# Mixture of softmaxes on one core: which output groups wait behind the last load, and where they wait

## The chip, the core and the metric

The kernel runs on one core of a Trainium2 chip. The metric is device time in microseconds (us) of one execution. Engines are PE (matmul; PEld is its weight load), DVE (vector), ACT (scalar), POOL (GpSimd) and SP (sync). Transfers between HBM (the chip's main memory) and SBUF (on-chip memory of 128 partitions) are issued by SP and ACT in this kernel. Each of the two has its own queue, and both queues are served by the same 16 transfer engines.

## The reference, cut to what matters

```
prior_probs = softmax(prior, axis=-1)              # [32, 128, 4]
softmax     = softmax(logits, axis=-1)             # [32, 128, 4, 4096]
mixture     = sum over 4 heads of prior_probs[..., None] * softmax
```

The logits are 268 MB of float32, the output is 67 MB. For each of 4096 rows there are four heads of 4096 logits each. The result is one row of 4096 numbers: the four softmaxes, weighted by the softmax of four prior numbers.

## The kernel before, in words

**Tiling.** The 4096 rows are cut into G = 32 groups of 128 rows, and each group into J = 2 units of M = 64 rows, so there are N = 64 units. Unit n is half j = n % 2 of group n // 2. The four heads of a unit's 64 rows lie on 128 partitions: partition 2m + q holds heads 2q and 2q + 1 of row m, as two stretches of 4096 (Q = 2, index i). A unit is 4 MB, 32 KB on each partition.

**Loads.** `load(n)` (L66 to L72) is issued by SP, as one transfer of 4 MB; unit 63 alone is loaded as two of 2 MB. `slot(n)` (L63, L64) says in which of five slot tiles a unit lies: slot n % 5, except for the last six units, which go to slots 4, 0, 1, 2, 4, 0. Slot 3 is thus last read by unit 53. A slot can be loaded again when the matmuls of its earlier unit are done.

**Arithmetic of a unit.** `top(n, i)` (L74 to L81) takes the maximum of a stretch on DVE (L76) and then the exponential with its sum on ACT (L79), in place. `weigh(n, i)` (L83 to L98) takes the reciprocal of the sum on DVE (L84), builds on POOL (L86) a 128 x 64 matrix which adds the two partitions of a row, weighted by prior and reciprocal, and runs 16 matmuls (L93). They add both stretches of the unit into one PSUM tile of 128 x 2048: partitions 0 to 63 hold output columns 0 to 2047, partitions 64 to 127 columns 2048 to 4095. `evict(n)` (L112, L113) copies that on ACT to the home of the group, once its matmuls are done.

**Homes and stores.** `home(g)` (L108 to L110) is where the sums of group g wait: half g % 2 of the output tile `obuf`, or of slot 3 for the two held groups, 28 and 29 (`HOLD` = 28, L106). `part` (L100 to L104) stores one half c of the partitions of a group, which is one half of its columns: 1 MB in pieces of 8 KB. Up to group 27, `store(g)` issues both halves on ACT as soon as the group's second unit has been copied (L174, L175).

**Order of the work.** The order is written out by hand; every engine takes its instructions in the order in which the loop names them. Step n of the loop (L155 to L179) does: the maximum and exponential of unit n's first stretch; the second `weigh` of unit n - 1; the load into the slot that unit n - 1 frees; maximum and exponential of the second stretch of unit n, and its first `weigh`; the copy of unit n - 1; and the stores that follow from it.

**The end.** At step 62 the held groups are stored: their upper halves (c = 1) by ACT, after the first exponential of unit 62 (L158 to L160), their lower halves (c = 0) by SP, behind the two halves of load 63 in SP's queue (L166 to L168). Groups 30 and 31 go the same two ways: group 30 after the copy of unit 61, the first half of group 31 after that of unit 62 (L176 to L179), and the last unit in two pieces of 1024 columns, each copied and stored on both queues (L183 to L186).

**Semaphores.** Completions of transfers are counted on eight semaphores in turn, shared by both queues. So an engine that issues a transfer may first have to wait for an earlier transfer that used the same semaphore; the list of built instructions shows where it does.

Of the kernel before, what the change touches and what calls it, by code (L numbers as in the profile page):

```python
# [17 lines left out]
SLOTS = 5  # L18


@with_exitstack
def kernel(
    ctx: ExitStack,
    tc: tile.TileContext,
    logits: bass.AP,
    prior: bass.AP,
    out: bass.AP,
):
    nc = tc.nc
    B, S, H, V = logits.shape  # L30
    R = M * J
    G = B * S // R
    N = G * J
    W = V // 2
    assert G * R == B * S and G == 32 and H == 2 * Q and V == 8 * BANK


    lg = logits.rearrange("b s h v -> (b s) h v").rearrange(
        "(g m j) (q i) v -> g j m q (i v)", m=M, j=J, i=Q
    )  # L40
    ov = out.rearrange("b s v -> (b s) v").rearrange("(g m j) v -> g m j v", m=M, j=J)
    pv = prior.rearrange("b s h -> (b s) h").rearrange("(g r) h -> g r h", r=R)

    cpool = ctx.enter_context(tc.tile_pool(name="cpool", bufs=1))
    psum = ctx.enter_context(tc.tile_pool(name="psum", bufs=1, space=bass.MemoryType.PSUM))

    slots = [cpool.tile([P, Q, V], FP32, name=f"slot{i}") for i in range(SLOTS)]

    obuf = cpool.tile([P, J, V], FP32, name="obuf")
    accs = [psum.tile([P, W], FP32, name=f"acc{i}") for i in range(2)]  # L50

    sel = cpool.tile([P, M], FP32, name="sel")
    wts = [[cpool.tile([P, M], FP32, name=f"wt{k}{i}") for i in range(Q)] for k in range(2)]
    pr = cpool.tile([G, R, H], FP32, name="pr")
    pn = cpool.tile([G, J, Q, M, Q], FP32, name="pn")
    pmax = cpool.tile([G, R], FP32, name="pmax")
    pp = cpool.tile([P, J, Q, G], FP32, name="pp")
    nmax = [cpool.tile([P, N], FP32, name=f"nmax{i}") for i in range(Q)]
    dsum = [cpool.tile([P, N], FP32, name=f"dsum{i}") for i in range(Q)]
    rden = [cpool.tile([P, N], FP32, name=f"rden{i}") for i in range(Q)]  # L60


    def slot(n):  # L63
        return slots[n % SLOTS if n < N - 6 else (4, 0, 1, 2)[(n - N + 6) % 4]]  # L64

    def load(n):  # L66
        src = lg[n // J, n % J]
        for i in range(0, Q, Q if n < N - 1 else 1):
            k = Q if n < N - 1 else 1
            nc.sync.dma_start(  # L70
                out=slot(n)[:, i : i + k], in_=src[:, :, i * V : (i + k) * V]
            )  # L72

    def top(n, i):  # L74
        x = slot(n)[:, i]
        nc.vector.tensor_reduce(  # L76
            out=nmax[i][:, n : n + 1], in_=x, axis=AX.X, op=ALU.max, negate=True
        )
        nc.scalar.activation(  # L79
            x, x, AF.Exp, bias=nmax[i][:, n : n + 1], accum_out=dsum[i][:, n : n + 1]  # L80
        )  # L81

    def weigh(n, i):  # L83
        nc.vector.reciprocal(rden[i][:, n : n + 1], dsum[i][:, n : n + 1])  # L84
        wt = wts[n % 2][i]
        nc.gpsimd.tensor_scalar(  # L86
            out=wt, in0=sel, scalar1=rden[i][:, n : n + 1],
            scalar2=pp[:, n % J, i, n // J : n // J + 1], op0=ALU.mult, op1=ALU.mult,
        )

        for b in range(W // BANK):
            for c in range(2):
                nc.tensor.matmul(  # L93
                    accs[n % 2][c * M : (c + 1) * M, b * BANK : (b + 1) * BANK],
                    lhsT=wt,
                    rhs=slot(n)[:, i, c * W + b * BANK : c * W + (b + 1) * BANK],
                    start=i == 0, stop=i == Q - 1,
                )  # L98

    def part(eng, g, c, js=slice(0, J), lo=0, hi=W):  # L100
        eng.dma_start(  # L101
            out=ov[g, :, js, c * W + lo : c * W + hi],
            in_=home(g)[c * M : (c + 1) * M, js, lo:hi],
        )  # L104

    HOLD = G - 4  # L106

    def home(g):  # L108
        x = slots[3] if HOLD <= g < G - 2 else obuf
        return x[:, g % 2].rearrange("p (j w) -> p j w", j=J)  # L110

    def evict(n, lo=0, hi=W):  # L112
        nc.scalar.copy(home(n // J)[:, n % J, lo:hi], accs[n % 2][:, lo:hi])  # L113

    def store(g):
        for c in range(2):
            part(nc.scalar, g, c)

    def prior_user(n):
        return max(k for k in range(n) if slot(k) is slot(n))  # L120

    with tc.manual_schedule():
        for n in range(SLOTS):
            load(n)
        nc.scalar.dma_start(out=pr, in_=pv)

        nc.gpsimd.memset(sel, 1.0)  # L127
        nc.gpsimd.affine_select(  # L128
            out=sel, in_=sel, compare_op=ALU.is_ge, fill=0.0, base=0,
            pattern=[[-Q, M]], channel_multiplier=1,  # L130
        )
        nc.gpsimd.affine_select(  # L132
            out=sel, in_=sel, compare_op=ALU.is_ge, fill=0.0, base=Q - 1,
            pattern=[[Q, M]], channel_multiplier=-1,
        )

        nc.vector.reduce_max(pmax, pr, axis=AX.X)  # L137
        nc.vector.tensor_sub(pr, pr, pmax.unsqueeze(2).to_broadcast([G, R, H]))  # L138
        nc.scalar.activation(pr, pr, AF.Exp)  # L139
        nc.vector.reduce_sum(pmax, pr, axis=AX.X)  # L140
        nc.vector.reciprocal(pmax, pmax)  # L141
        prv = pr.rearrange("g (m j) (q i) -> g j i m q", j=J, i=Q)
        pmv = pmax.rearrange("g (m j) -> g j m", j=J)
        for j in range(J):
            for i in range(Q):
                nc.vector.tensor_mul(  # L146
                    pn[:, j, i], prv[:, j, i], pmv[:, j].unsqueeze(2).to_broadcast([G, M, Q])
                )
        pq = pn.rearrange("g j i m q -> g j i (m q)")
        for t in range(P // 32):  # L150
            nc.vector.transpose(  # L151
                pp[32 * t : 32 * (t + 1)], pq[:, :, :, 32 * t : 32 * (t + 1)]
            )

        for n in range(N):  # L155
            w = n - 1
            top(n, 0)
            if n == N - 2:  # L158
                for g in (HOLD, HOLD + 1):
                    part(nc.scalar, g, 1)  # L160
            if w >= 0:
                weigh(w, 1)
                for k in range(SLOTS, N):
                    if prior_user(k) == w:
                        load(k)
                if w == N - 3:  # L166
                    for g in (HOLD, HOLD + 1):
                        part(nc.sync, g, 0)  # L168
            top(n, 1)
            weigh(n, 0)  # L170
            if w >= 0:
                evict(w)
                g = w // J
                if w % J == J - 1 and g < HOLD:  # L174
                    store(g)  # L175
                elif w == N - 3 or w == N - 2:  # L176
                    js = slice(0, J) if w == N - 3 else slice(0, 1)
                    part(nc.sync, g, 0, js)
                    part(nc.scalar, g, 1, js)  # L179

        n = N - 1
        weigh(n, 1)
        for lo in (0, W // 2):  # L183
            evict(n, lo, lo + W // 2)
            part(nc.sync, n // J, 0, slice(1, 2), lo, lo + W // 2)
            part(nc.scalar, n // J, 1, slice(1, 2), lo, lo + W // 2)  # L186
# [30 lines left out]
```

## Time and profile before

| | |
|---|---|
| median of 3 runs | 792.72 us (790.87 to 792.88) |
| the profiled execution, own time | 793.28 us |
| its span (first to last instruction) | 791.6 us |
| mean granted clock of PE | 0.873 |
| busy: PE, DVE, ACT, POOL | 548.0, 573.3, 600.2, 51.6 us |
| read and written | 268.50 and 67.11 MB, 424 GB/s over the span |
| SP's queue (q1), share of the 16 transfer engines | 80.4% |
| ACT's queue (q10) | 19.1% |
| one maximum (L76), one exponential (L79), one full copy (L113) | 4.41, 3.71, 1.82 us |

The profile is of one execution. Its views are the page (busy shares, the span in 40 slices, queues, the chain of work that ended last, the costliest groups of instructions) and answers to questions: the busy time in chosen stretches, the instructions in order of time, the waits, and the transfers with their time from issue to landing. A unit's landing is read from the DVE maximum that waits for it: units 56 to 62 land at 686.8, 699.0, 711.1, 723.5, 735.25, 745.0 and 754.7 us.

### The profile page before, as it was taken

Reading aid. Unit: us, or ns where it says so; the run is one execution under the profiler, and the core shown is the slowest. Engines: PE = TensorE matmul, PEld = TensorE weight load, DVE = VectorE, ACT = ScalarE, POOL = GpSimd, SP = SyncE. Lnnn points to the kernel's source line nnn. Section 1 sums busy time; section 2 is a strip of 40 time slices with the busy share of each in tenths; the row PEclk is TensorE's granted clock in tenths of the full one; section 3 lists DMA queues with packets and bytes.
Section 4 is the critical chain, followed back from the end, with each engine's and each line's share of the span. In section 5 each row is a group of like instructions: output and inputs, shape, how many; then the busy total and the mean of one; then the engine's idle time right before and its main releaser. Section 6 shows DMA issues by size and latency. Waiting matters only on the chain.

```text
span 791.6 us, 5426 instructions
## 1 busy us (share of the span) xinstructions
PE 548.0 (69%) x2048; PEld 160.4 (20%) x2048; DVE 573.3 (72%) x268; ACT 600.2 (76%) x323; POOL 51.6 (7%) x135
## 2 busy tenths in 40 slices
PE   0777568776687765767766767677578776687884
PEld 0222112221122221222211222222122221122221
DVE  5986867767768668677686676776867867768890
ACT  1897777787787787877877778778777787787894
POOL 0000000000000000000000000000000000000000
PEclk9999997899978899888999798789997799977897
DMA  9999999999999999999999999999999999999997
GB/s 376 442 416 431 431 428 430 432 431 427 434 432 435 429 432 436 430 433 431 434 429 433 431 431 429 428 435 431 429 431 432 431 432 433 433 430 436 429 416 229
DMA packets 18841, 335.95 MB, mean 424 GB/s; under 512 B 2144, under 2 KB 2144, under 8 KB 2432
## 3 DMA queue, kind: packets, MB, share of 16 engines
q1 hardware_dynamic: 10032, 272.63, 80.4%
q10 hardware_dynamic: 8784, 62.98, 19.1%
q8 instruction: 16, 0.26, 0.1%
q14 instruction: 9, 0.07, 0.0%
HBM read 268.50 MB, written 67.11 MB: 424 GB/s over the span
## 4 chain that ended last, share of the span: by engine, by line
DMA 73%; PE 12%; DVE 10%; ACT 2%; issue 1%; POOL 1%; ACTq 0%; SPq 0%; POOLq 0%
DMA slot<-in_logits_dram 73%; PE acc L93 12%; DVE nmax L76 10%; ACT slot L79 1%; POOL wt L86 1%; ACT obuf L113 1%; ACTq L101 0%; DVE rden L84 0%; SPq L70 0%; POOLq L86 0%; ACTq L79 0%; ACTq L113 0%
## 5 line engine op out<-in xcount | busy, mean ns | idle before, releaser
L93 PE MATMUL acc<-slot,wt 128*64 128x512 f32 x2048 | 548.0, 693 | 235.3 <-POOL wt L86 235.3
L76 DVE TENSOR_REDUCE nmax<-slot 128x1 f32<-128x4096 f32 x128 | 563.5, 4410 | 194.6 <-DMA slot<-in_logits_dram 194.6
L79 ACT ACTIVATE slot<-slot,nmax 128x4096 f32<-128x4096 f32 x128 | 474.6, 3708 | 178.0 <-DVE nmax L76 175.4
L93 PEld LDWEIGHTS acc<-slot,wt 128*64 128x64 f32 x2048 | 160.4, 158 | 622.0 <-POOL wt L86 311.8
L113 ACT COPY obuf<-acc 128x2048 f32<-128x2048 f32 (+1 forms) x61 | 110.9, 1817 | 4.8 <-PE acc L93 4.2
L86 POOL TENSOR_SCALAR wt<-sel,rden,pp 128x64 f32<-128x64 f32 x128 | 50.8, 397 | 725.7 <-DVE rden L84 721.8
L84 DVE RECIPROCAL rden<-dsum 128x1 f32<-128x1 f32 x128 | 19.6, 153 | 6.0 <-ACT slot L79 6.0
L79 ACT ACTIVATION_READ_ACCUMULATOR slot<-slot,nmax 128x1 f32 x128 | 23.9, 186 | 0.0
L113 ACT COPY slot<-acc 128x2048 f32<-128x2048 f32 x4 | 7.4, 1844 | 0.0
L137 DVE TENSOR_REDUCE pmax<-pr 32x128 f32<-32x512 f32 x1 | 0.7, 674 | 2.7 <-DMA pr<-in_prior_dram 2.7
L139 ACT ACT_TABLE_LOAD x1 | 1.3, 1283 | 1.2 <-PEq L201 1.2
L139 ACT ACTIVATE pr<-pr 32x512 f32<-32x512 f32 x1 | 0.6, 628 | 1.6 <-DVE pr L138 1.6
L151 DVE STREAM_TRANSPOSE pp<-pn 32x128 f32<-32x128 f32 x4 | 1.2, 302 | 0.1
L140 DVE TENSOR_REDUCE pmax<-pr 32x128 f32<-32x512 f32 x1 | 0.7, 674 | 0.7 <-ACT pr L139 0.7
L141 DVE RECIPROCAL pmax<-pmax 32x128 f32<-32x128 f32 x1 | 0.9, 942 | 0.0
L146 DVE TENSOR_TENSOR pn<-pr,pmax 32x128 f32<-32x128 f32 x4 | 0.9, 274 | 0.0
L138 DVE TENSOR_TENSOR pr<-pr,pmax 32x512 f32<-32x512 f32 x1 | 0.7, 678 | 0.0
L128 POOL TENSOR_SCALAR_AFFINE_SELECT sel<-sel 128x64 f32<-128x64 f32 x1 | 0.2, 241 | 0.1
L132 POOL TENSOR_SCALAR_AFFINE_SELECT sel<-sel 128x64 f32<-128x64 f32 x1 | 0.2, 240 | 0.1
L127 POOL MEMSET sel<- 128x64 f32 x1 | 0.2, 153 | 0.3 <-POOLq L201 0.3
L201 POOL MEMSET const-float32-0.0<- 128x1 f32 x1 | 0.1, 99 | 0.3 <-issue 0.3
L201 POOL MEMSET const-bfloat16-1.0<- 128x1 bf16 x1 | 0.1, 102 | 0.0
(2 smaller groups left out, 0.2 us busy)
## 6 DMA issues: line engine op xcount, KB each, us to landing
slot<-in_logits_dram SPq DMA_DIRECT2D x63, 4096.0 KB, 38.0
out_dram<-obuf ACTq DMA_DIRECT2D x57, 1024.0 KB, 21.5
slot<-in_logits_dram SPq DMA_DIRECT2D x2, 2048.0 KB, 20.2
out_dram<-slot SPq DMA_DIRECT2D x2, 1024.0 KB, 24.3
out_dram<-slot ACTq DMA_DIRECT2D x2, 1024.0 KB, 12.2
out_dram<-obuf SPq DMA_DIRECT2D x1, 1024.0 KB, 11.2
out_dram<-obuf SPq DMA_DIRECT2D x1, 512.0 KB, 4.3
out_dram<-obuf ACTq DMA_DIRECT2D x1, 512.0 KB, 6.2
```

The costliest lines, as they stand in the source:

```text
L76: nc.vector.tensor_reduce(out=nmax[i][:, n : n + 1], in_=x, axis=AX.X, op=ALU.max, negate=True)
L79: nc.scalar.activation(x, x, AF.Exp, bias=nmax[i][:, n : n + 1], accum_out=dsum[i][:, n : n + 1])
L84: nc.vector.reciprocal(rden[i][:, n : n + 1], dsum[i][:, n : n + 1])
L86: nc.gpsimd.tensor_scalar(out=wt, in0=sel, scalar1=rden[i][:, n : n + 1], scalar2=pp[:, n % J, i, n // J : n // J + 1], op0=ALU.mult, op1= ...
L93: nc.tensor.matmul(accs[n % 2][c * M : (c + 1) * M, b * BANK : (b + 1) * BANK], lhsT=wt, rhs=slot(n)[:, i, c * W + b * BANK : c * W + (b + ...
L113: nc.scalar.copy(home(n // J)[:, n % J, lo:hi], accs[n % 2][:, lo:hi])
L137: nc.vector.reduce_max(pmax, pr, axis=AX.X)
L138: nc.vector.tensor_sub(pr, pr, pmax.unsqueeze(2).to_broadcast([G, R, H]))
L139: nc.scalar.activation(pr, pr, AF.Exp)
L141: nc.vector.reciprocal(pmax, pmax)
L146: nc.vector.tensor_mul(pn[:, j, i], prv[:, j, i], pmv[:, j].unsqueeze(2).to_broadcast([G, M, Q]))
L151: nc.vector.transpose(pp[32 * t : 32 * (t + 1)], pq[:, :, :, 32 * t : 32 * (t + 1)])
```

## The change

The five last units, instead of six, leave out a slot: they go to slots 0, 1, 2, 3, 0, and it is slot 4 that is left out, last read by unit 54. `HOLD` becomes 26, so four groups are held and stored at step 62 instead of two: 26 and 27 in the output tile, 28 and 29 in slot 4. Groups 30 and 31, which before used the output tile, go to the slot of unit 60 (slot 1). What is computed, the sizes of the transfers and the queues that they take are as before.

```diff
     def slot(n):
-        return slots[n % SLOTS if n < N - 6 else (4, 0, 1, 2)[(n - N + 6) % 4]]
+        return slots[n % SLOTS if n < N - 5 else (n - N + 5) % 4]

-    HOLD = G - 4
+    HOLD = G - 6

     def home(g):
-        x = slots[3] if HOLD <= g < G - 2 else obuf
+        x = obuf if g < G - 4 else slots[4] if g < G - 2 else slot(N - 4)
         return x[:, g % 2].rearrange("p (j w) -> p j w", j=J)

             if n == N - 2:
-                for g in (HOLD, HOLD + 1):
+                for g in range(HOLD, G - 2):
                     part(nc.scalar, g, 1)

                 if w == N - 3:
-                    for g in (HOLD, HOLD + 1):
+                    for g in range(HOLD, G - 2):
                         part(nc.sync, g, 0)
```

## The prediction, on record before the result

> **What bounds the kernel now.** I read the page's slices first, for whether one resource is full all the way and where it stops being full.
>
> ```profile
> DMA  9999999999999999999999999999999999999997
> GB/s 376 442 416 431 431 428 430 432 431 427 434 432 435 429 432 436 430 433 431 434 429 433 431 431 429 428 435 431 429 431 432 431 432 433 433 430 436 429 416 229
> ```
>
> The transfers fill every slice (19.8 us each) except the last, which moves 229 GB/s instead of some 430. All that can be won sits there; elsewhere only bytes or rate would help, and the change alters neither the bytes nor the size of their pieces. So the second view is the stretches of the end, cut where units land (columns: us, busy time with count for PE, PEld, DVE, ACT, POOL, then granted clock, DMA share, GB/s).
>
> ```profile
> 711.10:723.50 12.40, 10.35 (x42) 3.10 (x40) 8.89 (x5) 9.62 (x6) 0.79 (x2) 0.86 0.99 426
> ...
> 735.25:745.00 9.75, 7.75 (x30) 2.28 (x28) 8.88 (x5) 7.32 (x6) 0.79 (x2) 0.82 1.00 431
> 745.00:754.70 9.70, 8.02 (x38) 2.39 (x36) 8.87 (x5) 9.17 (x6) 0.79 (x2) 1.00 0.98 424
> 754.70:764.40 9.70, 7.30 (x34) 2.12 (x34) 9.70 (x5) 9.31 (x6) 0.79 (x2) 1.00 1.00 422
> 764.40:770.00 5.60, 4.87 (x24) 1.42 (x24) 5.60 (x3) 4.89 (x4) 0.40 (x1) 1.00 1.02 423
> 770.00:774.00 4.00, 2.26 (x12) 0.52 (x8) 2.44 (x2) 4.00 (x3) 0.00 (x1) 1.00 1.03 371
> 774.00:778.00 4.00, 3.55 (x10) 1.07 (x12) 0.16 (x1) 4.00 (x3) 0.71 (x2) 0.63 0.93 354
> 778.00:782.00 4.00, 4.00 (x20) 1.39 (x18) 0.00 (x0) 1.04 (x1) 0.09 (x1) 0.94 0.61 150
> 782.00:786.00 4.00, 1.23 (x6) 0.14 (x2) 0.00 (x0) 2.02 (x2) 0.00 (x0) 0.91 0.78 198
> 786.00:790.00 4.00, 0.00 (x0) 0.00 (x0) 0.00 (x0) 0.00 (x0) 0.00 (x0) 0.50 0.78 228
> ```
>
> A unit that shares the transfers with a store takes 12.1 to 12.4 us, one that has them alone 9.70 to 9.75. The last load ends near 764. The held stores then run at 423 GB/s until they run out around 774; from 778 on the rate is 150 to 228 GB/s, because the remaining stores wait for the arithmetic of units 62 and 63. The chain shows that arithmetic (start, us, what).
>
> ```profile
> 735.06 19.62 DMA slot<-in_logits_dram
> 754.70 4.42 DVE nmax L76
> ...
> 774.45 8.81 PE acc L93 x32
> 783.26 0.02 issue
> 783.28 1.02 ACT obuf L113
> ```
>
> Unit 62 lands at 754.68; its and unit 63's work ends with the last copy at 785.9, 31.2 us later. The last store lands at 790.5 and the span ends at 791.6, 1.1 us on.
>
> **The change, part by part.** Times are of this execution: span 791.6, 793.28 with what lies around it (1.7 us), which is 0.56 above the median 792.72.
>
> *Stores moved.* The four stores of groups 26 and 27 leave step 54 and 56 and stand behind the last load: 4 x 1.05 MB = 4.19 MB. Their two issues on ACT were at 677.0 and 701.27, with 26.2 and 26.4 us to landing, so they shared the transfers with units 57 to 60. Those four units lost 12.1 + 12.4 + 11.75 + 12.2 (the stretches between the landings at 686.8, 699.0, 711.1, 723.5 and 735.25) = 48.45 us against 4 x 9.72 = 38.9. So unit 60, and with it 61 to 63, lands 9.6 us earlier; 4.19 MB at the 431 GB/s of a stretch gives 9.7. I take 9.7: unit 62 at 745.0, last load ended near 754.7.
>
> *Can the arithmetic follow at 9.7 per unit?* DVE has 2 x 4.41 + 2 x 0.15 less overlap = 8.9 (the stretches say 8.87 and 8.88). ACT has 2 x 3.71 + 1.84 and its small reads = 9.3. PE has 32 matmuls, 7.30 at clock 1.00. All under 9.7, and units 61 and 62 already do it. I count nothing.
>
> *Slots.* Loads 59 to 63 reuse the slot of the unit four before, as before the change; 58 now has five. A load is released by the last matmuls of that unit, about 10.6 us after the next unit's landing (load 59 takes unit 55's slot; unit 56 landed at 686.8, load 59 was issued at 697.41). At 9.7 per landing it then still has 8.8 us of queued load ahead of it. Nothing, until PE is 8 us late.
>
> *Homes.* Groups 28 and 29 go to slot 4, last read by unit 54, 30 and 31 to the slot of unit 60, whose matmuls end before the copy of its sums. Copies to slots took 1844 ns, those to the output tile 1845. Nothing.
>
> *Issues and their waits.* ACT issues four held stores instead of two between the two exponentials of unit 62. The two took 0.55 and 0.79 from 759.25; four take 2.7, to 762.0, and the next exponential started at 763.54. Covered; beyond that each further issue would cost 0.6. The list of built instructions shows new waits, since the transfers share eight completion semaphores: the fourth held store on ACT waits for the first half of load 63 (4.9 us after unit 62, about when it is issued), and the store of group 30, which stands ahead of both exponentials of unit 63, waits for group 26's first store. The store in the same place in the queue before was issued at 759.25 with 9.6 to landing: 768.85, against 769.12 when the store of group 30 is issued. So 0.25 us to spare: I count 0, bounds 0 to 3, and cover exists (below). SP's waits stand ahead of nothing but stores.
>
> *The new end.* At 764.5 the trace has 7.53 MB of stores still to move. After, 7.53 + 4.19 = 11.72 MB at 754.8. No run shows so long a stretch of stores alone, so its rate is the unknown. Bounds: 423 (764.4 to 770, both queues full) and 354 to 371 (770 to 778). I take 423, since the later rows are those in which group 29's stores ran out and group 30's, issued at 769.12, were only arriving; in the changed kernel more is always queued. For the last 1.05 MB, in pieces of half the size, I take 360: 10.67/0.423 = 25.2, 1.05/0.36 = 2.9, so 782.9. Add 2.0 for engines that finish unevenly (the rate fell from 350 to 24 in four steps of 0.7 us near 778; bounds 1 to 2.7) and 1.1 to the end: span 786.0. The arithmetic's last copy comes at 785.9 - 9.7 = 776.2, and the last stores are wanted only at 782.9 - 2.9 = 780.0: 3.8 us of cover for all the nothings above. Time 786.0 + 1.7 = 787.7, by the median 787.1. The end would no longer be set by the chain of units 62 and 63 but by the store queues: a gain of 5.6 us, no more, though the last load moves by 9.7.
>
> A rule of the Trainium skill speaks against this. SBUF — State Buffer, "Can I just issue two DMAs to hit both halves?", answers no: two transfers, each from one half of the partitions, serialize, with a gain of 6% over one; a half reaches 218 GB/s. By it 11.72 MB would take 51 us and the kernel over 805 us. The row 764.4:770 has 423 GB/s with such halves on two queues, so I go by the row; where one queue stores alone (780 to 782) the trace has 197.
>
> **The rivals.**
>
> *A long run of stores is slower* (354 to 371 for all of it). For: the rows from 770. Against: DMA share is 1.03 at 371, but the queue mix changes there. 11.72/0.36 = 32.6, so 787.4 + 2.0 + 1.1 = 790.5 span, 791.6 by the median: no change.
>
> *The arithmetic becomes the bound.* The clock was 0.63 to 0.86 in several rows, and the 16 matmuls of half a unit then took 5.38 (at 691.98) instead of 3.65 (at 750.13): 10.8 per unit against 9.7. Seven such units in a row would put PE 7 us behind, 3 us past the cover: 790. At the mean clock 0.873 a unit takes 8.4 and nothing happens. Price 1 to 3 us: 788 to 790.
>
> *Halves fall out of step* (slower). Lower halves of the output go by SP's queue, upper ones by ACT's. If SP's four held stores ran first and ACT's after, each MB would go at 197 instead of 423: 5.3 instead of 2.5 us. ACT's wait ahead of unit 63 would then also bind. Four MB alone cost 11.4 us: 798.5; all eight 810. It passes the bound for slower (795.1) once 2.8 MB go alone. Against: the two held pairs landed at 768.85 and 769.9, 774.7 and 774.8, in step.
>
> *The units don't land earlier*, because loads wait for slots or something else: then the last load stays and all 11.72 MB start at 764.5: 764.5 + 28.1 + 2.0 + 1.1 = 795.7 span, 796.8 by the median. Against: 9.70 per unit with four slots in the rows above.
>
> **How the numbers follow.** Forecast 0.70 (785.0 to 789.5), slow stores 0.13, arithmetic 0.08, out of step 0.06, no earlier landing 0.03. Low end: 423 throughout, 1.0 uneven: 782.5 + 1.0 + 1.1 = 784.6 span, 785.7, and 0.7 for what isn't in the sum: 785.0. High end: the slow stores, 791.6, with 0.4 for the scatter of the runs: 792.0. A measurement can tell 0.3% (2.4 us) from no change: faster is under 790.3, which takes the forecast and most of the arithmetic case, 0.78; same 0.13; slower 0.09.
>
> **What would show it.** Right: landings every 9.7 us from 686.8 on, unit 62 near 745; after the last load a plateau near 420 GB/s until some 3 us before the end; no dip to 150. ACT's exponential of unit 63 starts within 1 us of the copy before it. Wrong: a plateau at 360 (slow stores), one queue alone at 200 (out of step), PE busy without gap from 700 on (arithmetic), or units still 12 us apart.

## The result, and the profile after

The changed kernel took 789.67 us (median of 6 runs, 789.23 to 790.35) against 792.8 for the kernel before on the same chip. The ratio is 0.9967, with a 95% interval of 0.9954 to 0.9980: a gain of 3.1 us, where the forecast was 5.6. The profiled execution took 789.42, with a span of 787.7. Timed again on another chip, the ratio was 0.9971 (0.9961 to 0.9982).

The first view is again the page's slices (19.7 us each), now of the changed kernel.

```profile
DMA  9999999999999999999999999999999999999998
GB/s 376 438 426 433 433 427 433 431 433 429 433 431 431 431 428 434 429 432 433 433 431 431 434 424 431 433 428 430 431 433 437 429 432 435 431 437 428 424 417 312
```

The last slice moves 312 GB/s instead of 229, but it is still far from 430. The stretches after the last load say why (columns as in the prediction: busy times, then granted clock, DMA share, GB/s):

```profile
745.00:754.70 9.70, 7.30 (x34) 2.12 (x32) 9.70 (x5) 9.30 (x6) 0.79 (x2) 1.00 0.99 421
754.70:760.00 5.30, 4.57 (x22) 1.35 (x20) 5.30 (x3) 4.69 (x4) 0.39 (x1) 1.00 1.02 430
760.00:765.00 5.00, 2.91 (x14) 0.87 (x12) 2.50 (x2) 5.00 (x3) 0.39 (x1) 0.94 1.00 411
765.00:770.00 5.00, 5.00 (x20) 1.41 (x18) 0.16 (x1) 4.00 (x3) 0.39 (x1) 0.72 1.02 397
770.00:775.00 5.00, 3.16 (x16) 0.83 (x12) 0.00 (x0) 1.20 (x2) 0.00 (x0) 1.00 1.01 380
775.00:780.00 5.00, 0.00 (x0) 0.00 (x0) 0.00 (x0) 0.82 (x1) 0.00 (x0) 0.80 1.01 368
780.00:784.00 4.00, 0.00 (x0) 0.00 (x0) 0.00 (x0) 0.00 (x0) 0.00 (x0) 0.50 0.94 330
```

There is no hole any more: the transfer engines are busy (share 1.0) to 780, and the arithmetic ends nearly 12 us before the span does, with a last copy that is done at 775.8. But the rate slides from 430 to 368 while the share stays at 1.0, and to 330 at a share of 0.94. The engines are not waiting for work; each byte takes longer. The records of single pieces of 8 KB agree: over the five rows from 754.7 to 780 one took 309, 316, 336, 346 and 360 ns in the mean, and 430 GB/s times 309/360 is 369, where the row has 368.

The units land as forecast. The maxima of DVE that wait for a landing (start, length, idle time before) stand 9.71 us apart:

```profile
696.20 4.42 DVE L76 TENSOR_REDUCE nmax<-slot 128x1 f32<-128x4096 f32 x1 [0.84 <-DMA slot<-in_logits_dram]
705.91 4.42 DVE L76 TENSOR_REDUCE nmax<-slot 128x1 f32<-128x4096 f32 x1 [0.83 <-DMA slot<-in_logits_dram]
...
744.75 4.42 DVE L76 TENSOR_REDUCE nmax<-slot 128x1 f32<-128x4096 f32 x1 [0.83 <-DMA slot<-in_logits_dram]
```

Unit 62 lands at 744.7, against 754.7 before and 745.0 forecast. On ACT, in order of time, the four held stores are issued from 749.2 to 752.3, ahead of the second exponential of unit 62 (753.60, which waits for DVE, as before). The exponential of unit 63 starts 0.6 us after the copy ahead of it, as before (0.7):

```profile
749.22 0.56 ACTq L101 DMA_DIRECT2D out_dram<-obuf  x1
...
749.80 0.74 ACTq L101 DMA_DIRECT2D out_dram<-obuf  x1
750.58 1.74 ACTq L101 DMA_DIRECT2D out_dram<-slot  x2
...
753.60 3.71 ACT L79 ACTIVATE slot<-slot,nmax 128x4096 f32<-128x4096 f32 x1 [0.40 <-DVE nmax L76]
...
759.17 0.54 ACTq L101 DMA_DIRECT2D out_dram<-slot  x1
759.76 3.71 ACT L79 ACTIVATE slot<-slot,nmax 128x4096 f32<-128x4096 f32 x1 [0.61 <-ACT slot L113]
...
774.81 1.01 ACT L113 COPY slot<-acc 128x1024 f32<-128x1024 f32 x1 [0.59 <-ACT slot L113]
```

So the open question was the sliding rate: is it the stores' reading of half the partitions, or any long run of writes?

### The profile page after: what moved, and what is told of

Its sections match the earlier page's. It is cut to its first block, busy times and chain, and to the rows that moved or that the text cites. A ratio compares the mean times of both kernels' runs of the same rounds, so it can differ in the third digit from the quotient of the medians.

```text
span 787.7 us, 5429 instructions
## 1 busy us (share of the span) xinstructions
PE 539.4 (68%) x2048; PEld 157.7 (20%) x2048; DVE 573.4 (73%) x268; ACT 599.8 (76%) x323; POOL 51.1 (6%) x135
## 4 chain that ended last, share of the span: by engine, by line
DMA 73%; PE 11%; DVE 10%; ACT 2%; issue 1%; POOL 1%; ACTq 0%; SPq 0%; POOLq 0%
DMA slot<-in_logits_dram 73%; PE acc L93 11%; DVE nmax L76 10%; ACT slot L79 1%; POOL wt L86 1%; ACT slot L113 0%; ACTq L101 0%; ACT obuf L113 0%; DVE rden L84 0%; SPq L70 0%; POOLq L86 0%; ACTq L79 0%
## 5 line engine op out<-in xcount | busy, mean ns | idle before, releaser
L93 PE MATMUL acc<-slot,wt 128*64 128x512 f32 x2048 | 539.4, 684 | 233.8 <-POOL wt L86 233.8
L93 PEld LDWEIGHTS acc<-slot,wt 128*64 128x64 f32 x2048 | 157.7, 156 | 614.6 <-POOL wt L86 313.8
L113 ACT COPY obuf<-acc 128x2048 f32<-128x2048 f32 x56 | 103.3, 1844 | 0.0
L113 ACT COPY slot<-acc 128x2048 f32<-128x2048 f32 (+1 forms) x9 | 14.9, 1658 | 4.8 <-PE acc L93 4.2
```

The costliest lines, as they stand in the source:

```text
L93: nc.tensor.matmul(accs[n % 2][c * M : (c + 1) * M, b * BANK : (b + 1) * BANK], lhsT=wt, rhs=slot(n)[:, i, c * W + b * BANK : c * W + (b + ...
```

## The experiments

Theory 1: a store of this kernel reads 64 partitions, one half. Engines that read the same half at the same time hold each other up, and two queues that begin in opposite halves drift into reading the same one at the same moments ("in step" in the expectations; the prediction calls it in step when the two queues share the transfers evenly). Theory 2: writes to HBM that run alone for long are slower, whatever they read. The twelve kernels were timed in three groups on three chips, each beside the kernel before, whose medians there were 791.57, 791.65 and 791.48.

### Stores over all 128 partitions

```diff
     def part(eng, g, c, js=slice(0, J), lo=0, hi=W):
+        if HOLD <= g < G - 1:
+            eng.dma_start(out=oc[g, c * P : (c + 1) * P], in_=home(g)[:, c])
+            return
```

(`oc[g]` is the group's output as 256 pieces of 8 KB in order.)

> The changed kernel, but the stores of groups 26 to 30 are cut by the unit (j) and not by the half of the partitions (c): each of them reads 128 partitions of one 8 KB row each and writes 128 pieces of 8 KB, one after the other in the output. Number, size and queue of the stores are as in the changed kernel; the numbers of groups 26 to 30 land at other places of the output. Theory 1 (halves of the partitions: a store of 64 partitions reaches only part of the ways into SBUF, and two queues that drift into step slow each other): the rate after the last load stays at 420 or more until the last 2 MB, the store-only stretch is 12.6 MB / 0.42 = 30 us instead of 33, and the time is 3 us under the changed kernel, about 786.5. Theory 2 (writes to HBM that run alone for over 10 us are slower, whatever they read): the rate falls to 380 and 350 from about 10 us after the last load as in the changed kernel, and the time stays at 789.7 within 0.8.

Measured: 787.55, ratio 0.9944 (0.9927 to 0.9960), 4.0 us under the kernel before, where the changed kernel was 3.1 and, timed again, 1.9 under it. By the ratios it is 1.8 to 2.1 us faster than the changed kernel, less than the 3 expected. Its stretches:

```profile
760.00:765.00 5.00, 2.17 (x12) 0.43 (x7) 2.35 (x2) 4.39 (x3) 0.20 (x1) 1.00 1.02 433
765.00:770.00 5.00, 4.71 (x22) 1.54 (x24) 0.16 (x1) 4.85 (x3) 0.59 (x2) 1.00 1.00 423
770.00:775.00 5.00, 2.60 (x14) 0.57 (x8) 0.00 (x0) 1.77 (x2) 0.00 (x0) 1.00 1.01 426
775.00:780.00 5.00, 0.00 (x0) 0.00 (x0) 0.00 (x0) 0.26 (x1) 0.00 (x0) 0.70 1.02 413
```

The same number of bytes and stores, written alone for the same time, doesn't slow down until group 31, whose stores were left as halves. In the records of single 8 KB pieces none before 776 took over 0.4 us (309 ns each), where in the changed kernel 12 of 94 did between 768 and 770 and 21 of 83 between 778 and 780. Theory 2 falls: a run of writes as long kept its rate. These stores also wrote without gaps; the kernels with long and short pieces below take that up. The span is 786.0, which is the sum of the prediction; that it agrees to the tenth is in part luck, since group 31 slowed down here too.

### Both queues on the same half

```diff
-                for g in range(HOLD, G - 2):
-                    part(nc.scalar, g, 1)
+                for c in range(2):
+                    for g in range(HOLD + 2, G - 2):
+                        part(nc.scalar, g, c)
...
-                    for g in range(HOLD, G - 2):
-                        part(nc.sync, g, 0)
+                    for c in range(2):
+                        for g in range(HOLD, HOLD + 2):
+                            part(nc.sync, g, c)
```

> The changed kernel, but the eight held stores are dealt out anew: SP stores the lower halves of groups 26 and 27 and then their upper halves, ACT the same of groups 28 and 29, so both queues read the same half of the partitions at a time. Theory 1: 4.2 MB go at 200 to 215 GB/s, 20 us, and the other 4.2 MB as well, against 20 us for all of it before: 15 to 20 us slower, 805 to 810. Theory 2: no change, 789.7 within 0.8.

Measured: 807.17, ratio 1.0194 (1.0179 to 1.0209), 15.6 us over the kernel before and some 18, by the ratios, over the changed one.

```profile
756.00:764.00 8.00, 5.47 (x20) 1.48 (x18) 6.30 (x3) 5.49 (x3) 0.40 (x1) 0.80 1.01 220
764.00:772.00 8.00, 4.90 (x24) 1.45 (x22) 0.51 (x3) 7.61 (x5) 0.40 (x1) 0.99 0.99 272
772.00:780.00 8.00, 4.34 (x20) 1.05 (x16) 0.08 (x1) 2.64 (x2) 0.40 (x1) 1.00 0.99 219
```

On the same half, the two queues get 220 GB/s with a DMA share of 1.0: of the 215 pieces begun between 756 and 764, 186 took 0.55 to 0.64 us instead of 0.309. The 272 of the middle row is likely the change from the lower to the upper halves; no record shows which half a piece was read from. The kernel before is much the same where SP's queue stores alone, from 780 to 782: 197 GB/s, and all 48 pieces took over 0.4 us, half of them 0.628 or more. The changed kernel, at 330 and more, stays well above this. The Trainium skill (SBUF — State Buffer, "Door 1: The DMA port swizzle") has a half of the partitions reach 8 of 16 ports, some 218 GB/s, and 220 agrees.

### Long pieces, and short ones

```diff
     def part(eng, g, c, js=slice(0, J), lo=0, hi=W):
+        if HOLD <= g < G - 1:
+            eng.dma_start(
+                out=oc[g, c * P : (c + 1) * P].rearrange("(m j) w -> m j w", j=J),
+                in_=home(g)[c * M : (c + 1) * M],
+            )
+            return
```

> The changed kernel, with stores of 64 partitions as there, but each of the 1 MB stores of groups 26 to 30 writes one stretch of 1 MB of the output instead of pieces of 8 KB with gaps of 8 KB; the numbers land at other places. Theory 1 (halves of the partitions): no change, 789.7 within 0.8, rate falling to 380 and 350. Theory 2 in the form that the pattern of the writes in HBM is slow: faster, about 786.5, with 420 or more to the end. Theory 2 in the form that any long run of writes is slow: no change.

Measured: 794.59, ratio 1.0035 (1.0022 to 1.0048), 3 us over the kernel before: none of the three expectations. In the trace the stores had turned into pieces of 16 KB, since two neighbouring 8 KB rows now lie next to each other on both sides, so this kernel changed two things. The rate is down to 338 from 760 on:

```profile
760.00:765.00 5.00, 2.98 (x16) 0.92 (x14) 2.51 (x2) 5.00 (x3) 0.40 (x1) 1.00 0.96 338
765.00:770.00 5.00, 4.96 (x25) 1.49 (x22) 0.16 (x1) 3.95 (x3) 0.40 (x1) 1.00 1.03 341
770.00:775.00 5.00, 1.70 (x8) 0.29 (x4) 0.00 (x0) 2.02 (x2) 0.00 (x0) 0.92 0.99 338
```

The pattern in HBM is now without gaps, and it is slower, though the longer pieces could hide a gain. It suggested that engines hold each other up piece by piece, so that a shorter piece would hold up less. The next kernel stores 4 KB pieces from the same halves.

```diff
+        if HOLD <= g < G - 1:
+            eng.dma_start(
+                out=oy[g, :, :, c],
+                in_=home(g)[c * M : (c + 1) * M].rearrange("m j (y w) -> m (j y) w", y=2),
+            )
+            return
```

(`oy[g]` is a row pair's columns as quarter rows, y and c.)

> The changed kernel, but the stores of groups 26 to 30 write pieces of 4 KB with gaps of 4 KB instead of 8 KB with gaps of 8 KB; number, bytes, queues and halves of the partitions of the stores are the same, and the numbers land at other places inside their group. If engines that serve the same half hold each other up piece by piece, a smaller piece holds up less, as the 16 KB pieces of the earlier run held up more (340 GB/s): the rate after 10 us of stores alone stays at 395 to 410 instead of 380, time 0.5 to 2 us under the changed kernel. If the fall has another cause, a 4 KB piece only costs its own overhead (0.159 us against 0.155 for half of a 0.309 us piece, 3% of 30 us): 0.5 to 1 us over it.

Measured: 787.92, ratio 0.9951 (0.9938 to 0.9963), 1.8 us under the changed kernel, timed beside it:

> The changed kernel itself, timed on the same chip as the three that follow. All theories: 0.4% under the kernel before on this chip, within 0.15%.

Measured: 789.75, ratio 0.9971 (0.9961 to 0.9982). No run of the one overlaps a run of the other (787.58 to 788.04, 789.16 to 789.99). The stretches of the kernel with 4 KB pieces:

```profile
765.00:770.00 5.00, 4.96 (x24) 1.49 (x22) 0.16 (x1) 3.88 (x3) 0.39 (x1) 1.00 1.03 422
770.00:775.00 5.00, 1.63 (x8) 0.29 (x4) 0.00 (x0) 2.02 (x2) 0.00 (x0) 1.00 1.03 424
775.00:780.00 5.00, 0.00 (x0) 0.00 (x0) 0.00 (x0) 0.00 (x0) 0.00 (x0) 0.64 1.03 388
```

Over 770 to 775 the three lengths of piece give 338 (16 KB), 380 (8 KB) and 424 (4 KB). The halves were the same in all three. Gaps in HBM are thus not the cause: stores of halves were slow without gaps (16 KB) and kept their rate with them (4 KB). No run stored halves in 8 KB pieces without gaps.

### The homes alone

```diff
-    HOLD = G - 6
+    HOLD = G - 4
```

> One part of the change alone: slots and homes are those of the changed kernel (28 and 29 in slot 4, 30 and 31 in the slot of unit 60), but groups 26 and 27 are stored as soon as they are copied, as before. The theory of the prediction (only the bytes behind the last load count): the time of the kernel before, 792.8 within 0.8, and the units land 12 us apart up to unit 60. Rival (the homes themselves save or cost waits): over 1 us away from 792.8.

Measured: 791.40, ratio 0.9996 (0.9986 to 1.0005). The slots and homes are worth nothing by themselves; the deferral is all of the gain.

### Three held groups

```diff
-    HOLD = G - 6
+    HOLD = G - 5
```

> The changed kernel with three held groups, 27 to 29, instead of four: group 26 is stored as soon as it is copied. The units then land 4.9 us earlier than before instead of 9.7; 10.5 MB of stores stand behind the last load instead of 12.6 (8.4 before). Theory 1 (the store queues set the end, and their rate falls the longer they run alone, 425 at first and 380 and less after 10 us): the end comes at about 785.3 + 1.1, 0.5 to 1.3 us under the changed kernel, and the arithmetic's last copy, at 781, is still ahead of the last store. Rival (each held group is worth the same): half of the gain, so 1.5 us over the changed kernel. Rival (three groups leave too little cover and the arithmetic sets the end again): level with the changed kernel, with a dip of the transfers ahead of the last stores.

Measured: 788.98 against 789.75 for four held groups on the same chip, ratio to the kernel before 0.9964 (0.9950 to 0.9977). The medians are 0.8 us apart, but the two intervals overlap; that three is better than four is likely, not settled. That the gain is not proportional to the groups held is settled: half of it would be 790.7, outside the interval.

### Arithmetic taken away, after and before

The last 16 matmuls are left out, once in the changed kernel and once in the kernel before.

```diff
+        if n == N - 1 and i:
+            return
         for b in range(W // BANK):
...
-                    start=i == 0, stop=i == Q - 1,
+                    start=i == 0, stop=i == Q - 1 or n == N - 1,
```

> The changed kernel without the last 16 matmuls (the second stretch of unit 63 is not added to the sums), so that the last copies come 3.7 to 5 us earlier. If the store queues set the end (the prediction's new bound): no change, within 0.4 us of the changed kernel. If the arithmetic of units 62 and 63 still sets it: 3.5 to 5 us faster.

Measured: 789.47, ratio 0.9972 (0.9960 to 0.9983), against 789.75: no change. After the change, the store queues set the end.

> The kernel before without the last 16 matmuls (the second stretch of unit 63 is not added). The arithmetic set its end: 3 to 5 us faster than the kernel before, where the same edit of the changed kernel gave 0.3 us. Rival (the stores set the end before as well): within 0.8 us of the kernel before.

Measured: 791.10 against 791.48, ratio 0.9987 (0.9978 to 0.9996): 0.4 us where 3 to 5 were expected. The copies did come earlier, by 4.2 us against the profile before, whose last matmuls ran at a low clock, and by 2.7 us against that of the homes alone, where they ran at full clock (ACT, kernel before without the matmuls):

```profile
776.67 1.84 ACT L115 COPY obuf<-acc 128x2048 f32<-128x2048 f32 x1
...
780.70 1.01 ACT L115 COPY obuf<-acc 128x1024 f32<-128x1024 f32 x1 [0.59 <-ACT obuf L115]
```

but the span ended at 789.2, 7.5 us after this copy (781.7), where in the kernel before 5.7 us lie between the last copy (785.9) and the end. Group 31's 2.1 MB cannot start before unit 62 is copied, near 779, and then move slowly:

```profile
778.00:782.00 4.00, 0.00 (x0) 0.00 (x0) 0.00 (x0) 2.53 (x3) 0.00 (x0) 1.00 0.75 182
782.00:786.00 4.00, 0.00 (x0) 0.00 (x0) 0.00 (x0) 0.00 (x0) 0.00 (x0) 0.56 0.94 295
```

So the end before was set by the arithmetic up to unit 62 and by slow stores behind it. This follows from the order of the stores; no run took unit 62's work away. Of the 4.2 us, 2.4 reached the end (span 791.6 before), of the 2.7 us 0.9 (span 790.1), and 0.4 us show in the medians.

### Short pieces at their right places

For groups 26 to 31 the columns are dealt out anew: the lower half of the partitions sums the first and third quarter, the upper half the second and fourth. A store then writes quarter rows of 4 KB to where they belong.

```diff
+    def col(n, c, b):
+        if n // J < HOLD:
+            return c * W + b * BANK
+        return b // 2 * W + c * W // 2 + b % 2 * BANK
...
-                    rhs=slot(n)[:, i, c * W + b * BANK : c * W + (b + 1) * BANK],
+                    rhs=slot(n)[:, i, col(n, c, b) : col(n, c, b) + BANK],
...
+        if g >= HOLD:
+            y = slice(js.start * 2 + lo * 2 // W, (js.stop - 1) * 2 + hi * 2 // W)
+            eng.dma_start(
+                out=oy[g, :, y, c],
+                in_=home(g)[c * M : (c + 1) * M].rearrange(
+                    "m j (y w) -> m (j y) w", y=2
+                )[:, y],
+            )
+            return
```

> The changed kernel with 4 KB pieces put at their right places: for groups 26 to 31 the lower half of the partitions takes the first and third quarter of the columns and the upper half the second and fourth (only the columns that a matmul reads are dealt out anew), so that each 1 MB store writes 256 pieces of 4 KB. Theory (small pieces keep two engines on one half from holding each other up): 420 GB/s from the last load to the end, 11.7 MB / 0.42 = 27.9 us from 754.8, 1 to 1.5 us for uneven engines and 1.1 to the end: span 785, time 786.0 to 787.5, 2.3 to 3.7 us under the changed kernel. Rival (only the stretch before 776 gains, the end is set by something else): level with the run that had 4 KB pieces at wrong places, 1.8 us under the changed kernel.

Measured: 787.02, ratio 0.9939 (0.9926 to 0.9951), 4.5 us under the kernel before and the fastest of all; by the ratios it is 2.2 to 2.5 us under the changed kernel. Its span was 785.3; the sum had said 785.

> As the kernel with right places of 4 KB pieces, with three held groups instead of four. Theory: the queues would end 1.2 MB of rate difference earlier at best, but the arithmetic's last copy comes at 781 and its store lands 4.6 us later, 1.1 to the end: span 786.7, so 0.5 to 1.7 us slower than with four held groups, the reverse of the order found with 8 KB pieces. Rival (three held groups are better whatever the pieces): 0.8 us faster than with four.

Measured: 787.77, ratio 0.9946 (0.9932 to 0.9960). The medians stand in the order that was expected, 0.75 us apart, but the intervals overlap, and its last copy came at 779.3, not 781: unsettled.

> The kernel before (two held groups, its slots and homes) with 4 KB pieces for groups 28 to 31. Theory (before the change the arithmetic of units 62 and 63 sets the end, so the rate of the stores is worth little): within 0.8 us of the kernel before. Rival (the pieces are the gain, the deferral is not needed): 1.5 us or more under the kernel before.

Measured: 791.19, ratio 0.9998 (0.9989 to 1.0007). Two of its rows stand beside the 371 and 354 of the kernel before:

```profile
770.00:774.00 4.00, 1.82 (x10) 0.46 (x8) 1.83 (x2) 4.00 (x3) 0.39 (x1) 1.00 1.01 396
774.00:778.00 4.00, 3.96 (x18) 1.09 (x18) 0.17 (x1) 4.00 (x3) 0.39 (x1) 1.00 0.88 350
```

Short pieces without the deferral are worth nothing, the deferral with 8 KB pieces 0.3%, and both together 0.6%.

## Why the prediction was right in its direction and wrong in its size

**Right.** Deferring 4.19 MB moves the landings by that many bytes at the full rate (9.7 forecast, 9.95 measured at unit 62). The arithmetic follows at 9.7 per unit. ACT's four issues and its new waits cost nothing. The hole before the last stores is gone, and the end passes to the store queues: taking 16 matmuls away changes nothing after the change. The gain is much smaller than the shift of the last load.

**The step that failed** is in "The new end": "I take 423, since the later rows are those in which group 29's stores ran out and group 30's ... were only arriving; in the changed kernel more is always queued." In the changed kernel more was always queued, and the rate fell all the same, to 411, 397, 380, 368 and 330. The row of 371 in the profile before was slow pieces already: 29 of its 181 took over 0.4 us, against 5 of 289 in the row of 423, and with 4 KB pieces it was 396. Its share of 1.03 spoke against empty queues; the prediction names that share, beside a change of the queue mix, and does not follow it up. The row of 354 was empty queues as well, since with 4 KB pieces it stayed at 350, at a share of 0.88. From 754.7, 11.7 MB took until 786.6 (1.1 us before the span's end), 31.9 us against 30.1 in the sum, so the span was 787.7 instead of 786.0. With stores of all 128 partitions in place of the halves, the sum's span of 786.0 came out. The rival "a long run of stores is slower" had the fall of the rate right and its cause wrong, and the measured time lies between it and the forecast. "Halves fall out of step" was priced, at 11 us and more, as one queue that stores alone. That did not happen: from 754.7 on the two queues moved 5.90 and 5.78 MB. But it named the right property, stores of half the partitions. That the two queues drift onto the same half, and so hold each other up, is inferred from the runs with all partitions, with one half and with short pieces; no record shows the drift itself.

**The second mis-sized term** is the step from span to median. I took 0.56 off, since the profiled execution before was that much above its median. In that execution the last 32 matmuls took 8.78 us, at a granted clock of 0.63 from 774 to 778; in the run with the homes alone, with the same start, they took 7.34 at a clock of 1.00, and the span was 790.1:

```profile
774.44 7.34 PE L93 MATMUL acc<-slot,wt 128*64 128x512 f32 x32 [2.18 <-POOL wt L86]
```

An end that hangs on those matmuls scatters with the clock (790.87 to 793.11 before). The 21 runs of the kernel before beside the last group of experiments show it: 12 took 791.01 to 791.50 and 9 took 792.53 to 793.00, while without the last 16 matmuls all 11 runs took 790.86 to 791.39. The median before falls on one side or the other, which is also why the gain is 3.1 us on one chip and 1.9 on another. The end after does not hang on them, and its profile stood 0.25 below the median: 0.8 us between the two. Together 1.7 + 0.8 make 2.5 of the 2.6 us from 787.1 to 789.67; the rest is rounding.

**Wrong without showing in the number**: "the chain of units 62 and 63" did not set the end before as a whole. Unit 62's part did, by the order of the stores; unit 63's last 16 matmuls were worth 0.4 us, and some 1.5 more when the clock was low. Nor did the rates of 150 to 228 come from waiting alone: from 780 to 782 SP's queue was busy at a share of 0.93 and moved 197 GB/s, in pieces of 0.628 us.

## What to carry to other kernels

When a change moves bytes behind the last load, work the new end out with the rate of stores alone, and look in the trace for the longest stretch of them: a rate that falls while the DMA share stays at 1.0 is not a queue that runs dry. Here it was transfers that took longer each. In this kernel stores that read half of the partitions did no harm beside loads of all 128 (426 GB/s from 711 to 723 before) and slowed down beside each other; shorter pieces, or stores over all partitions, kept the rate until group 31's 8 KB halves were left. A scatter of the time before that comes from its own last steps must not be carried over to a kernel that ends on something else.

## What the runs showed of the hardware that was not expected

Two queues that store opposite halves begin at 423 to 430 GB/s, the full rate of this kernel, and slide to 380 in 15 to 20 us and to 330 at the end; on one half they get 220. The Trainium skill's SBUF — State Buffer ("Can I just issue two DMAs to hit both halves?") says no, with 6% more than one. Here the two got 430 and 411 GB/s in the first 10 us, nearly twice the 220 of one half, and 330 at the end, so the page's rule holds for neither end of the slide. The length of the piece decides how far it slides: 338, 380 and 424 GB/s for 16, 8 and 4 KB over the same 5 us. Why shorter pieces hold each other up less was not tried further: the trace shows that the long pieces stop occurring, not which engine waits for which. A store whose rows lie next to each other on both sides was turned into pieces of twice the length, although the access pattern that asked for it still names rows of 8 KB: in the run with long pieces the trace has 640 more pieces of 16 KB, which is ten stores of 64.
